# A first expert with 64 slots instead of 128 in a mixture-of-experts stage that streams its weights

## The chip, the cores and the metric

The kernel runs on one core of a Trainium2 chip. The time is device microseconds (us) of that core, the median of several executions of the whole program; less is better. Five engines work side by side: TensorE (PE, with its weight loads as PEld), VectorE (DVE), ScalarE (ACT), GpSimd (POOL) and SyncE (SP), which issues the DMA transfers here.

## The reference

A trunk of two layers over 256 latent tokens and 256 context tokens, model width 1024. The second layer ends with a top-2-of-8 mixture of SwiGLU experts on the 256 latent tokens, and this is the stage of the change:

```python
def _moe(h, router, w1, w3, w2):
    logits = (h @ router).astype(jnp.float32)
    top_v, top_i = lax.top_k(logits, TOP_K)
    weights = jax.nn.softmax(top_v, axis=-1)
    ...
    for e in range(N_EXPERTS):
        out = out + combine[..., e:e + 1] * _swiglu(h, w1[e], w3[e], w2[e])
    return out
```

An expert has three matrices of 1024 x 2816 in fp32, 34.6 MB together; all eight have 277 MB. The arithmetic of the reference on its inputs gives expert 0 54 of the 256 tokens, and the others, from most to least, 115, 83, 79, 58, 50, 46 and 27.

## The kernel before, in words

Only the tokens that chose an expert are computed for it. They are gathered into slots: a token's place in its expert gives a one-hot matrix (`onehot`), and TensorE multiplies the tokens by it (`gather`, tile `pgat`). An expert has either 128 slots ("big") or 64 ("small").

The two kinds are computed in different ways. A **big** expert splits every weight piece of 128x1024 into a high and a low part (`split`: `wh` on ACT, line 154, `wl` on DVE, line 155) and makes three products of 512 columns for each in place of one in full precision (lines 1229 to 1231 up, 1288 to 1290 down). A **small** expert takes the fp32 weights as they were loaded, unsplit, in two halves of 64 slots that lie beside each other in the array (line 1241 up, line 1296 down).

Expert 0 stands at position 0, whatever its count, so that its weights can be loaded before the router is done. The other seven are sorted by their counts (`route_sort`): positions 1 to 3 are big, 4 to 7 small. If more tokens chose an expert than it has slots, `over` is above zero, and a branch at the end computes everything once more for the tokens that were left over. `SEQ` is the order in which the positions are computed.

An expert runs in 11 steps (`NMC`) over its hidden width. A step takes three chunks of weights of 1 MB (tile `mraw`): two for the up product (tile `s`), one for the down product (tile `y`). On PE a step is the up product of this step, then the down product of the step before, then the turn of this step's hidden values (`pht`). The last step of an expert is followed by its combination into the output (`pcmb`), spread over the steps of the next. The gather of the next experts and their weights for the combination (`slots`, tile `ppw`) stand between the steps of a small expert.

The 264 chunks come through one queue on SP in the order of their use, into a ring of 14 buffers (`RINGA` 9, `RINGB` 5): the transfer of a chunk is issued when the buffer of the chunk 14 places ahead has been freed. A small expert frees a chunk when PE has multiplied by it, a big one when it has been split. The first 14 chunks are loaded while the mixer and the router still work. The ids of the experts after position 0 are read from `eid` by SP, ahead of the first chunk of the second expert.

```python
SEQ = (0, 4, 1, 5, 2, 6, 3, 7)
BIG = 4
CAPS = tuple(CAP if p < BIG else HALF for p in range(NE))
```

Of the kernel before, what the change touches and what calls it, by code (L numbers as in the profile page):

```python
# [13 lines left out]
P = 128  # L14
# [3 lines left out]
TC = 256  # L18
# [25 lines left out]

def _moe_order():
    order = []
    for n in range(NMS + 1):
        if n < NMS:
            order += [(n // NMC, n % NMC * 3 + q) for q in range(2)]
        if n:  # L50
            order.append(((n - 1) // NMC, (n - 1) % NMC * 3 + 2))
    return order


MOE_ORDER = _moe_order()


# [74 lines left out]
class Trunk:  # L132
# [808 lines left out]
    def mfetch(self):  # L941
        n = self.mi % len(MOE_ORDER)
        pool = self.mrawa if n % (RINGA + RINGB) < RINGA else self.mrawb
        t = pool.tile([P, MCH], F32, tag="mraw", name="mraw")
        s, j = MOE_ORDER[n]
        if s == 0:
            src = self.wm[j]
        else:
            if s not in self.eids:
                self.eids[s] = self.nc.values_load(  # L950
                    self.eid[0:1, SEQ[s]:SEQ[s] + 1], engines=[mybir.EngineType.SP], min_val=0, max_val=NE - 1,
                    skip_runtime_bounds_check_because="a sum over one row of a permutation of 0 to 7")
            src = self.wm.rearrange("(e j) p m -> e j p m", e=NE)[bass.ds(self.eids[s], 1), j].squeeze(0)
        self.nc.sync.dma_start(t, src)
        self.mi += 1
        self.mq.append(t)
# [55 lines left out]
    def route_end(self):  # L1012
# [49 lines left out]
        for tt, (hi, lo) in enumerate(self.tok):  # L1062
            for hf in range(2):
# [3 lines left out]
                self.order(ins, self.last_oh)  # L1067
        self.gate = self.last_act, ins.name
        return oh
# [62 lines left out]
    def moe(self, X):  # L1132
        tc, nc = self.tc, self.nc
        xe, self.eids = {}, {}
# [4 lines left out]
        def run():  # L1139
            self.experts(X, xe)  # L1140
# [23 lines left out]
    def onehot(self, es, pos=None):  # L1164
        pos = self.poss if pos is None else pos
        oh = []
        for tt in range(2):
            p = self.mp.tile([P, 2, P], F32R, tag="oh", name="oh", bufs=2)
            for q, e in enumerate(es):
                ins = self.nc.vector.tensor_scalar(p[:, q], self.v("iota" if e < BIG else "iota2", 0, P),  # L1170
                                                   pos[:, tt, e:e + 1], None, op0=ALU.is_equal).ins
            oh.append(p.rearrange("p a b -> p (a b)"))
        self.last_oh = ins.name
        for q, e in enumerate(es):
            self.oh[e] = [p[:, q * P:(q + 1) * P].bitcast(F32) for p in oh]
        return oh

    def gather(self, es, xe, oh):
        nc, mp = self.nc, self.mp
        n = P * len(es)  # L1180
        for e in es:
            if e < BIG:
                xe[e] = [(self.mtok if s else mp).tile([P, KD, P], F32R, tag=f"xe{s}", name=f"xe{s}", bufs=XB)
# [3 lines left out]
        for h in range(4):  # L1187
            ks = slice(2 * h, 2 * h + 2)
            for s in range(2):
# [6 lines left out]
                for q, e in enumerate(es):  # L1196
                    if e < BIG:
                        ins = nc.scalar.activation(xe[e][s][:, ks, :], pv[:, q], AF.Copy).ins
                    elif s == 0:
                        nc.scalar.activation(xe[e][:, ks, :], pv[:, q, :, 0:HALF], AF.Copy)  # L1200
                    else:
# [5 lines left out]
    def slots(self, e):  # L1207
# [5 lines left out]
        for tt in range(2):  # L1213
            nc.tensor.matmul(pt[:, TC:TC + NE], p[tt], self.comb[:, tt, :], start=(tt == 0), stop=(tt == 1))
        oht = mp.tile([P, TC], F32R if e < BIG else F32, tag="oht", name="oht", bufs=3)
        nc.vector.tensor_copy(oht, pt[:, 0:TC])
        ws = mp.tile([P, 2], F32, tag="ws", name="ws", bufs=3)
        nc.vector.tensor_copy(ws[:, 0:1], pt[:, TC + e:TC + e + 1])
        return oht, ws[:, 0:1]
# [123 lines left out]

    def experts(self, X, xe):
        pw, py = {}, {}
        self.last_down = None
        steps = [(s, c) for s in range(NE) for c in range(NMC)]
        prev = tail = None
        for n in range(len(steps) + 2):
            if n < len(steps):  # L1350
                s, c = steps[n]
                e = SEQ[s]
                big = e < BIG
                if c == 0:
# [4 lines left out]
                if n == len(steps) - 1:  # L1359
                    self.preload(AF.Sqrt)  # L1360
                if n == 2:
                    pw[e] = self.slots(e)
                at = (c - 4 if s == 0 else c - 1 if not big else -1)
                es = [SEQ[q] for q in (s + 1, s + 2)[:1 if s == 0 else 2] if q < NE]
                if at == 0 and es:
                    oh = self.onehot(es)
                elif at == 2 and es:
                    for _ in self.gather(es, xe, oh):
                        pass
                elif at == 4:  # L1370
                    for q in es:
                        pw[q] = self.slots(q)
                if s == 1 and c == NMC - 1 and self.over is None:
                    self.over = self.nc.values_load(self.cint[0:1, 0:1], min_val=0, max_val=2 * TC)
            else:
                new = None
            if prev:
                pe, pc, ph = prev
                if n == 1:
                    ph = self.turn_big(ph)  # L1380
                big = pe < BIG
# [6 lines left out]
            prev = new if n == 0 else (*new[:2], (self.turn_big if new[0] < BIG else self.turn_small)(new[2])) if new else None  # L1388
        while tail:
# [109 lines left out]
```

## Time and profile before

| | |
|---|---|
| median of 3 runs | 1870.61 us (1870.54 to 1872.69) |
| profiled execution, its own time | 1872.05 us |
| its span, first to last instruction | 1870.3 us |
| mean granted clock of TensorE | 0.991 |
| PE busy | 1831.2 us (98%) |
| DVE busy | 1300.2 us (70%) |
| ACT busy | 889.9 us (48%) |
| chunks of expert weights | 264 of 1024 KB |

The span is what the profiler saw between the first and the last instruction. The share of PE is an average over the whole trunk; the stage of the change is the part from about 1180 us to the end. GB/s in a row is what the core's 16 DMA engines moved together.

### The profile page before, as it was taken

How to read it: one execution, taken by the hardware profiler on the slowest of the kernel's cores; microseconds unless marked ns; L12 is line 12 of the kernel's file. 1: busy time of each engine (PE TensorE's matmuls, PEld its weight loads, DVE VectorE, ACT ScalarE, POOL GpSimd, SP SyncE). 2: the span in 40 equal slices, each digit the busy share in tenths (PEclk: the TensorE clock that was granted, in tenths of full speed). 3: DMA queues.
4: the chain of work that ended last, by engine and by line, in shares of the span. 5: the costliest groups of instructions: out<-in, count | busy, mean ns of one | idle time of the engine just before them, and what ended most of it. 6: DMA issues, size and time to landing. Idle time of an engine off the chain costs nothing.

```text
span 1870.3 us, 26861 instructions
## 1 busy us (share of the span) xinstructions
PE 1831.2 (98%) x10328; PEld 1420.8 (76%) x10328; DVE 1300.2 (70%) x2296; ACT 889.9 (48%) x1259; POOL 0.8 (0%) x6
## 2 busy tenths in 40 slices
PE   7999999999999999999999999999999999999997
PEld 4667777778998888889788998886577668667853
DVE  4899996355679967756999564984298259518932
ACT  3695332253552222235788553773177147416811
POOL 0000000000000000000000000000000000000000
PEclk8999999999999999999999999999999999999999
DMA  8233444231245555421243447789999999999993
GB/s 360 98 142 117 175 180 180 90 135 46 96 161 203 194 183 199 158 90 46 107 153 136 180 181 322 289 339 389 418 420 401 398 419 420 397 407 420 419 397 152
DMA packets 65655, 449.64 MB, mean 240 GB/s; under 512 B 7280, under 2 KB 7408, under 8 KB 23024
## 3 DMA queue, kind: packets, MB, share of 16 engines
q1 hardware_dynamic: 65520, 447.85, 61.1%
q8 instruction: 83, 1.36, 0.3%
q14 instruction: 52, 0.43, 0.1%
HBM read 446.78 MB, written 1.05 MB: 239 GB/s over the span
## 4 chain that ended last, share of the span: by engine, by line
PE 86%; DVE 10%; ACT 2%; DMA 1%; issue 1%; SPq 0%; ACTq 0%; DVEq 0%
PE ps L281 11%; PE ps L283 11%; PE ps L282 11%; PE s L1241 8%; PE s L1231 4%; PE y L1296 4%; PE s L1229 4%; PE s L1230 4%; DVE wl L155 2%; PE y L1290 2%; PE y L1288 2%; PE y L1289 2%; PE ps L780 2%; PE ps L779 2%; PE ps L781 2%; PE pcol L292 1%
## 5 line engine op out<-in xcount | busy, mean ns | idle before, releaser
L154 ACT ACTIVATE wh<-raw 128x1024 fp32r<-128x1024 f32 (+1 forms) x237 | 246.7, 1053 | 453.8 <-PE ps L282 287.1
L155 DVE TENSOR_TENSOR wl<-raw,wh 128x1024 fp32r<-128x1024 f32 (+1 forms) x237 | 286.3, 1215 | 131.5 <-ACT wh L154 129.1
L155 DVE TENSOR_TENSOR wl<-mraw,wh 128x1024 fp32r<-128x1024 f32 x264 | 314.4, 1222 | 29.9 <-ACT wh L154 23.8
L154 ACT ACTIVATE wh<-mraw 128x1024 fp32r<-128x1024 f32 x264 | 272.6, 1057 | 47.2 <-PE s L1230 33.0
L281 PE MATMUL ps<-nh,wh 128*128 128x512 f32 (+1 forms) x736 | 273.3, 371 | 0.7 <-ACT wh L154 0.7
L283 PE MATMUL ps<-nh,wl 128*128 128x512 f32 (+1 forms) x736 | 269.6, 367 | 3.1 <-DVE wl L155 3.1
L282 PE MATMUL ps<-nl,wh 128*128 128x512 f32 (+1 forms) x736 | 269.5, 366 | 0.0
L281 PEld LDWEIGHTS ps<-nh,wh 128*128 128x128 f32 x736 | 139.2, 189 | 30.7 <-issue 2.2
L1241 PE MATMUL s<-mraw,xes 128*64 128x256 f32 x1408 | 162.0, 380 | 0.0
L283 PEld LDWEIGHTS ps<-nh,wl 128*128 128x128 f32 x736 | 139.1, 189 | 27.7 <-DVE wl L155 3.3
L282 PEld LDWEIGHTS ps<-nl,wh 128*128 128x128 f32 x736 | 139.2, 189 | 25.3 <-issue 1.4
L257 ACT ACTIVATE hd<-s 128x256 f32<-128x256 f32 (+1 forms) x88 | 28.8, 328 | 242.5 <-PE s L1241 218.6
L1231 PE MATMUL s<-wl,xe 128*128 128x512 f32 x352 | 139.4, 396 | 4.2 <-DVE wl L155 4.2
L1229 PE MATMUL s<-wh,xe 128*128 128x512 f32 x352 | 142.0, 403 | 0.0
L1230 PE MATMUL s<-wh,xe 128*128 128x512 f32 x352 | 137.8, 392 | 0.0
L1241 PEld LDWEIGHTS s<-mraw,xes 128*64 128x64 f32 x1408 | 98.3, 137 | 44.9 <-issue 0.7
L1250 DVE TENSOR_TENSOR hd<-hd,s 128x256 f32<-128x256 f32 (+1 forms) x88 | 30.9, 351 | 129.9 <-ACT hd L257 129.9
L604 DVE SCALAR_TENSOR_TENSOR cv<-v,vec,cv 128x251 f32<-128x251 f32 (+14 forms) x240 | 102.4, 469 | 0.7
L233 DVE SCALAR_TENSOR_TENSOR junk<-wv,scr 128x512 f32<-128x512 f32 x128 | 84.1, 685 | 0.2
L1231 PEld LDWEIGHTS s<-wl,xe 128*128 128x128 f32 x352 | 66.4, 189 | 23.2 <-DVE wl L155 9.2
L1296 PE MATMUL y<-mraw,hs 128*64 128x512 f32 x352 | 83.4, 595 | 0.4 <-DVE hs L1275 0.4
L1229 PEld LDWEIGHTS s<-wh,xe 128*128 128x128 f32 x352 | 66.6, 189 | 13.0 <-ACT wh L154 0.6
(290 smaller groups left out, 3544.2 us busy)
## 6 DMA issues: line engine op xcount, KB each, us to landing
mraw<-in_wm_dram SPq DMA_DIRECT2D x264, 1024.0 KB, 9.5
raw<-in_wd_dram SPq DMA_DIRECT2D x64, 2048.0 KB, 7.8
wv<-in_wv_dram SPq DMA_DIRECT2D x96, 256.0 KB, 3.6
lw<-in_wd_dram SPq DMA_DIRECT2D x16, 256.0 KB, 2.8
raw<-in_wd_dram SPq DMA_DIRECT2D x2, 1024.0 KB, 14.4
xs<-in_xt_dram SPq DMA_DIRECT2D x1, 1024.0 KB, 4.9
xc<-in_xt_dram SPq DMA_DIRECT2D x1, 1024.0 KB, 7.3
scr<-in_sr_dram SPq DMA_DIRECT2D x4, 256.0 KB, 8.6
```

Of the source, the lines that this page charges most:

```text
L154: return (self.nc.scalar.activation(hi, src, AF.Copy), self.nc.vector.tensor_tensor(lo, src, hi.bitcast(F32), op=ALU.subtract))
L155: self.nc.vector.tensor_tensor(lo, src, hi.bitcast(F32), op=ALU.subtract))
L233: nc.vector.scalar_tensor_tensor(junk, w[h], 1.0, rows[2 * s + h], op0=ALU.mult, op1=ALU.mult, accum_out=acc[:, h, s:s + 1])
L281: self.nc.tensor.matmul(o, wh, ah, start=(k == 0), stop=False)
L282: self.nc.tensor.matmul(o, wh, al, start=False, stop=False)
L283: self.nc.tensor.matmul(o, wl, ah, start=False, stop=(k == KD - 1))
L604: nc.vector.scalar_tensor_tensor(cv[:, a0:a1], v[:, a0 + d:a1 + d], w(t), cv[:, a0:a1], op0=ALU.mult, op1=ALU.add)
L1229: nc.tensor.matmul(p1, xe[0][:, k, :], wh[:, cs], start=(k == 0), stop=False)
L1230: nc.tensor.matmul(p1, xe[1][:, k, :], wh[:, cs], start=False, stop=False)
L1231: nc.tensor.matmul(p1, xe[0][:, k, :], wl[:, cs], start=False, stop=(k == KD - 1))
L1241: nc.tensor.matmul(p1[r, 0:2 * P].rearrange("p (g f) -> p g f", g=2), xe[:, k, :], w[:, :, h * P:(h + 1) * P], start=(k == 0), stop=(k == ...
L1296: ins = self.nc.tensor.matmul(py[0][r, :], hs[:, f * HALF:(f + 1) * HALF], raw[:, f * PIECE + q * 512:f * PIECE + (q + 1) * 512], start=(c ...
```

## The change

Position 0 gets 64 slots: three big positions (1, 2, 3) and five small ones are left. The order becomes small, big, small, big, small, big, small, small. For the overflow there is a second order of nine rounds, `SEQ2`, in which position 0 has two rounds of 128 slots; the branch gathers each expert by itself (`alone`). The order `gate` on the first splits after the gather goes away.

```diff
-SEQ = (0, 4, 1, 5, 2, 6, 3, 7)
-BIG = 4
-CAPS = tuple(CAP if p < BIG else HALF for p in range(NE))
+SEQ = (0, 1, 4, 2, 5, 3, 6, 7)
+BIG = (1, 2, 3)
+CAPS = tuple(CAP if p in BIG else HALF for p in range(NE))
+SEQ2 = (0, NE, 1, 2, 3, 4, 5, 6, 7)
+BIG2 = (0, NE, 1, 2, 3)
...
-        self.gate = self.last_act, ins.name
...
         self.over = None
-        run()
+        run(SEQ)
         with tc.If(self.over > 0):
-            nc.vector.tensor_tensor(self.poss, self.poss,
+            more = self.mp.tile([P, 2, NE + 1], F32, tag="more", name="more")
+            nc.vector.tensor_tensor(more[:, :, 0:NE], self.poss,
                                     self.v("caps", 0, NE).unsqueeze(1).to_broadcast([P, 2, NE]), op=ALU.subtract)
-            for _ in self.gather((0,), xe, self.onehot((0,))):
-                pass
-            run()
+            nc.vector.tensor_scalar(more[:, :, NE], more[:, :, 0], -float(CAP), None, op0=ALU.add)
+            self.poss, self.bigs = more, BIG2
+            run(SEQ2, True)
...
                 at = (c - 4 if s == 0 else c - 1 if not big else -1)
-                es = [SEQ[q] for q in (s + 1, s + 2)[:1 if s == 0 else 2] if q < NE]
+                es = [] if alone else [seq[q] for q in (s + 1, s + 2) if q < NE][:1 if s + 1 < NE and seq[s + 1] not in self.bigs else 2]
```

What this does to the engines' order shows at three places. On PE, right after the first gather, the up product of expert 0 stood as triples of 512 columns; before:

```order
L1193 MATMUL pgat<-oh,tkh 128x128 x4
L1193 MATMUL pgat<-oh,tkl 128x128 x4
L1229 MATMUL s_10534<-wh,xe_10435 128x512
L1230 MATMUL s_10534<-wh,xe_10436 128x512
L1231 MATMUL s_10534<-wl,xe_10435 128x512
L1229 MATMUL s_10534<-wh,xe_10435 128x512
L1230 MATMUL s_10534<-wh,xe_10436 128x512
L1231 MATMUL s_10534<-wl,xe_10435 128x512
```

The same place on PE with the change (its line numbers are 2 higher; `s`, `pht`, `y` and `ppw` as above):

```order
L1195 MATMUL pgat<-oh,tkh 128x128 x4
L1195 MATMUL pgat<-oh,tkl 128x128 x4
L1243 MATMUL s_10532<-mraw,xes 64x256 x16
L1243 MATMUL s_10552<-mraw,xes 64x256 x16
L1271 MATMUL pht<-vec,hd 64x128 x2
L1298 MATMUL y<-mraw,hs 64x512 x4
L1271 MATMUL pht<-vec,hd 64x128 x2
L1243 MATMUL s_10586<-mraw,xes 64x256 x16
L1214 MATMUL ppw<-vec,oh 128x128 x2
```

The products read the loaded chunks (`mraw`) where they read split pieces, and an up product is 16 products of 256 columns for 64 slots where it was 24 of 512 columns.

On DVE after the tokens' low part (`tkl`), the splits of expert 0 (`wl`) stood between the rows of `route_sort`; before:

```order
L1065 TENSOR_TENSOR tkl<-tk,tkh 128x512 x4
L1079 COPY cnt<-ppos 128x8
L155 TENSOR_TENSOR wl<-mraw,wh 128x1024
L1080 TENSOR_TENSOR led<-cnt,vec 128x8
L155 TENSOR_TENSOR wl<-mraw,wh 128x1024
L1084 TENSOR_TENSOR G_10492<-led 128x64
L1085 TENSOR_TENSOR E_10493<-led 128x64
L155 TENSOR_TENSOR wl<-mraw,wh 128x1024
```

The same place on DVE with the change:

```order
L1067 TENSOR_TENSOR tkl<-tk,tkh 128x512 x4
L1080 COPY cnt<-ppos 128x8
L1081 TENSOR_TENSOR led<-cnt,vec 128x8
L1204 TENSOR_TENSOR xes<-xes,pgat 128x128
L1085 TENSOR_TENSOR G_10491<-led 128x64
L1086 TENSOR_TENSOR E_10492<-led 128x64
L1087 TENSOR_TENSOR E_10492<-E_10492,vec 128x64
L1088 TENSOR_TENSOR G_10491<-G_10491,E_10492 128x64
L1204 TENSOR_TENSOR xes<-xes,pgat 128x128
```

The splits are gone from here, and four additions that finish the small expert's gathered tokens (`xes`) have come in.

On PE where the last expert (position 7) begins: before, it followed a big expert, whose last down product and four parts of its combination (`pcmb`, line 1320) stand in its first steps:

```order
L1241 MATMUL s_15631<-mraw,xes 64x256 x16
L1296 MATMUL y<-mraw,hs 64x512 x4
L1320 MATMUL pcmb<-oht,yh 128x256
L1320 MATMUL pcmb<-oht,yl 128x256
L1320 MATMUL pcmb<-oht,yh 128x256
L1320 MATMUL pcmb<-oht,yl 128x256
L1269 MATMUL pht<-vec,hd 64x128 x2
L1241 MATMUL s_15673<-mraw,xes 64x256 x8
```

With the change it follows position 6, a small one, whose combination is one row:

```order
L1243 MATMUL s_15163<-mraw,xes 64x256 x16
L1298 MATMUL y<-mraw,hs 64x512 x4
L1339 MATMUL pcmb<-oht,ys 128x256 x8
L1271 MATMUL pht<-vec,hd 64x128 x2
L1243 MATMUL s_15218<-mraw,xes 64x256 x16
L1298 MATMUL y<-mraw,hs 64x512 x4
L1271 MATMUL pht<-vec,hd 64x128 x2
```

So the last two experts run through one kind of step without a change of kind between them. On SP the order is the same in both: 32 chunks, the read of `eid`, and the rest.

## Rows read from the trace of the kernel before

**Rows 1.** The page: its span, and the chain that ended last by engine.

```profile
span 1870.3 us, 26861 instructions
...
PE 86%; DVE 10%; ACT 2%; DMA 1%; issue 1%; SPq 0%; ACTq 0%; DVEq 0%
```

**Rows 2.** Windows, one an expert: busy us by engine, PEclk, DMA share, GB/s.

```profile
1180.00:1277.00 97.00, 96.89 (x452) 78.83 (x450) 87.80 (x116) 76.33 (x92) 0.00 (x0) 0.99 0.88 335
1277.00:1347.00 70.00, 70.00 (x550) 42.45 (x550) 14.75 (x46) 10.10 (x29) 0.00 (x0) 1.00 1.01 411
1347.00:1444.00 97.00, 95.61 (x430) 75.32 (x428) 85.80 (x94) 70.22 (x85) 0.00 (x0) 1.00 1.01 418
1444.00:1516.00 72.00, 70.61 (x552) 42.22 (x550) 16.41 (x46) 11.66 (x30) 0.00 (x0) 1.00 0.98 396
...
1783.00:1840.00 57.00, 55.63 (x438) 32.41 (x438) 12.73 (x31) 5.96 (x14) 0.00 (x0) 1.00 0.95 386
```

**Rows 3.** Tile mraw: issues (ns min/median/max, first and last start us); issue to landing.

```profile
L954 SPq DMA_DIRECT2D mraw<-in_wm_dram x264: 327/333/642, 1127.1 to 1825.3; - x132
...
DMA to landing us min/median/max: 4.7/9.5/22.8
```

**Rows 4.** Timeline of PE, expert 0 begins: start us, us, instruction.

```profile
1179.52 0.74 PE L1229 MATMUL s<-wh,xe 128*128 128x512 f32 x1
...
1181.76 0.48 PE L1231 MATMUL s<-wl,xe 128*128 128x512 f32 x1
1182.08 0.39 PE L1229 MATMUL s<-wh,xe 128*128 128x512 f32 x1
```

**Rows 5.** Timeline of PE, first up product of positions 4, 5 and 7; in brackets idle before.

```profile
1276.96 3.67 PE L1241 MATMUL s<-mraw,xes 128*64 128x256 f32 x32
...
1444.19 3.67 PE L1241 MATMUL s<-mraw,xes 128*64 128x256 f32 x32
1449.19 0.50 PE L1288 MATMUL y<-wh,hh 128*128 128x512 f32 x1 [1.32 <-ACT wh L154]
...
1782.82 3.67 PE L1241 MATMUL s<-mraw,xes 128*64 128x256 f32 x32
```

**Rows 6.** Timeline of PE, big step: down product begins, two following up products begin.

```profile
1373.76 0.39 PE L1288 MATMUL y<-wh,hh 128*128 128x512 f32 x1
...
1376.63 0.48 PE L1229 MATMUL s<-wh,xe 128*128 128x512 f32 x1
...
1385.06 0.48 PE L1229 MATMUL s<-wh,xe 128*128 128x512 f32 x1
```

**Rows 7.** Timeline of PE, one small step and the next one's start.

```profile
1330.43 3.62 PE L1241 MATMUL s<-mraw,xes 128*64 128x256 f32 x32
1333.88 1.89 PE L1296 MATMUL y<-mraw,hs 128*64 128x512 f32 x8
...
1335.82 3.62 PE L1241 MATMUL s<-mraw,xes 128*64 128x256 f32 x32
```

**Rows 8.** Chain in order of time: start us, us on the chain, work.

```profile
1235.72 3.62 PE pgat L1193 x32
...
1289.12 0.67 PE pcmb L1320 x4
...
1299.81 4.03 PE pgat L1193 x32
...
1366.16 1.92 PE pcmb L1337 x14
```

**Rows 9.** Timeline of PE, slots of two experts, and what follows them.

```profile
1316.34 0.44 PE L1212 MATMUL ppw<-vec,oh 128*128 128x128 f32 x2
...
1317.67 1.94 PE L1296 MATMUL y<-mraw,hs 128*64 128x512 f32 x8
```

**Rows 10.** Timeline of PE, the last down product of the last expert.

```profile
1849.12 1.94 PE L1296 MATMUL y<-mraw,hs 128*64 128x512 f32 x8 [0.39 <-DVE hs L1275]
```

More of the change, by code (lines that the diff above doesn't have):

```diff
@@ L42, with _moe_order @@
 RINGA, RINGB, XB = 9, 5, 1
[L45 to L51, printed above, removed]
+def _moe_order(seq):
+    order, n = [], len(seq) * NMC
+    for m in range(n + 1):
+        if m < n:
+            order += [(seq[m // NMC], m % NMC * 3 + q) for q in range(2)]
+        if m:
+            order.append((seq[(m - 1) // NMC], (m - 1) % NMC * 3 + 2))
     return order
-MOE_ORDER = _moe_order()
+MOE_ORDER = _moe_order(SEQ) + _moe_order(SEQ2)
 def _vec_layout():
@@ L941, in mfetch @@
     def mfetch(self):
-        n = self.mi % len(MOE_ORDER)
+        n = self.mi
         pool = self.mrawa if n % (RINGA + RINGB) < RINGA else self.mrawb
         t = pool.tile([P, MCH], F32, tag="mraw", name="mraw")
-        s, j = MOE_ORDER[n]
-        if s == 0:
+        e, j = MOE_ORDER[n]
+        if e % NE == 0:
             src = self.wm[j]
         else:
-            if s not in self.eids:
-                self.eids[s] = self.nc.values_load(
-                    self.eid[0:1, SEQ[s]:SEQ[s] + 1], engines=[mybir.EngineType.SP], min_val=0, max_val=NE - 1,
+            if e not in self.eids:
+                self.eids[e] = self.nc.values_load(
+                    self.eid[0:1, e:e + 1], engines=[mybir.EngineType.SP], min_val=0, max_val=NE - 1,
                     skip_runtime_bounds_check_because="a sum over one row of a permutation of 0 to 7")
-            src = self.wm.rearrange("(e j) p m -> e j p m", e=NE)[bass.ds(self.eids[s], 1), j].squeeze(0)
+            src = self.wm.rearrange("(e j) p m -> e j p m", e=NE)[bass.ds(self.eids[e], 1), j].squeeze(0)
         self.nc.sync.dma_start(t, src)
@@ L1133, in moe @@
         tc, nc = self.tc, self.nc
-        xe, self.eids = {}, {}
+        xe, self.eids, self.bigs = {}, {}, BIG
         for _ in self.gather((0,), xe, self.route_end()):
@@ L1138, in moe, with run @@
         self.route_weights()
-        def run():
-            self.experts(X, xe)
+        def run(*what):
+            self.experts(X, xe, *what)
             rs = self.rstd_cols(self.colsum(self.square(X, TC, T, "rt"), TC, "rt"), TC)
@@ L1181, in gather @@
         for e in es:
-            if e < BIG:
+            if e in self.bigs:
                 xe[e] = [(self.mtok if s else mp).tile([P, KD, P], F32R, tag=f"xe{s}", name=f"xe{s}", bufs=XB)
@@ L1196, in gather @@
                 for q, e in enumerate(es):
-                    if e < BIG:
+                    if e in self.bigs:
                         ins = nc.scalar.activation(xe[e][s][:, ks, :], pv[:, q], AF.Copy).ins
                     elif s == 0:
-                        nc.scalar.activation(xe[e][:, ks, :], pv[:, q, :, 0:HALF], AF.Copy)
+                        ins = nc.scalar.activation(xe[e][:, ks, :], pv[:, q, :, 0:HALF], AF.Copy).ins
                     else:
@@ L1214, in slots @@
             nc.tensor.matmul(pt[:, TC:TC + NE], p[tt], self.comb[:, tt, :], start=(tt == 0), stop=(tt == 1))
-        oht = mp.tile([P, TC], F32R if e < BIG else F32, tag="oht", name="oht", bufs=3)
+        oht = mp.tile([P, TC], F32R if e in self.bigs else F32, tag="oht", name="oht", bufs=3)
         nc.vector.tensor_copy(oht, pt[:, 0:TC])
         ws = mp.tile([P, 2], F32, tag="ws", name="ws", bufs=3)
-        nc.vector.tensor_copy(ws[:, 0:1], pt[:, TC + e:TC + e + 1])
+        nc.vector.tensor_copy(ws[:, 0:1], pt[:, TC + e % NE:TC + e % NE + 1])
         return oht, ws[:, 0:1]
@@ L1342, in combine_small, with experts @@
         yield
-    def experts(self, X, xe):
+    def experts(self, X, xe, seq, alone=False):
         pw, py = {}, {}
         self.last_down = None
-        steps = [(s, c) for s in range(NE) for c in range(NMC)]
+        steps = [(s, c) for s in range(len(seq)) for c in range(NMC)]
         prev = tail = None
@@ L1351, in experts @@
                 s, c = steps[n]
-                e = SEQ[s]
-                big = e < BIG
+                e = seq[s]
+                big = e in self.bigs
+                if alone and c == 0:
+                    oh = self.onehot((e,))
+                    pw[e] = self.slots(e)
+                    for _ in self.gather((e,), xe, oh):
+                        pass
                 if c == 0:
@@ L1360, in experts @@
                     self.preload(AF.Sqrt)
-                if n == 2:
+                if n == 2 and not alone:
                     pw[e] = self.slots(e)
                 at = (c - 4 if s == 0 else c - 1 if not big else -1)
-                es = [SEQ[q] for q in (s + 1, s + 2)[:1 if s == 0 else 2] if q < NE]
+                es = [] if alone else [seq[q] for q in (s + 1, s + 2) if q < NE][:1 if s + 1 < NE and seq[s + 1] not in self.bigs else 2]
                 if at == 0 and es:
@@ L1369, in experts @@
                         pass
-                elif at == 4:
+                elif at == 4 and es:
                     for q in es:
                         pw[q] = self.slots(q)
-                if s == 1 and c == NMC - 1 and self.over is None:
+                if n == 2 * NMC - 1 and self.over is None:
                     self.over = self.nc.values_load(self.cint[0:1, 0:1], min_val=0, max_val=2 * TC)
@@ L1378, in experts @@
                 pe, pc, ph = prev
+                big = pe in self.bigs
                 if n == 1:
-                    ph = self.turn_big(ph)
-                big = pe < BIG
+                    ph = (self.turn_big if big else self.turn_small)(ph)
                 (self.down_big if big else self.down_small)(py[pe], self.mnext(), ph, pc)
```

4 lines of the change are left out of this document (2 added, 2 removed).

## The prediction

> **What bounds the kernel now.** I read the page first: PE holds 86% of the chain that ended last, DMA 1% [rows 1]. That share covers the whole trunk, so I took the expert stage apart next, with windows cut where one expert ends and the next begins [rows 2]. The reader is to see two things there. PE is busy in every stretch (96.89 of 97 us in expert 0, 70.00 of 70 in position 4). And the DMA engines look just as full (share 0.98 to 1.01 after the first expert), yet move different amounts: 335 GB/s in expert 0, 411 to 418 in the next two, 396 in the fourth. A queue that always had a free buffer to fill would not do that. So PE sets the pace, and the weights are close behind it. A gain on PE counts, until the weights become the later of the two; the sum needs both.
>
> **The first expert, big to small.** Expert 0 runs on PE from 1179.52 [rows 4] to 1276.96 [rows 5], where position 4 begins: 97.4 us. As a small one it would take:
> - 11 steps of 5.39 us (1330.43 to 1335.82), less the last down product and turn, which belong to the next expert's stretch (1333.88 to 1335.82, 1.94 us): 57.4 us [rows 7].
> - One gather for two experts, 4.03 us; before it was for one, 3.62 us [rows 8].
> - Slots: for its own 0.7 and for two 1.3 us (1316.34 to 1317.67 for two [rows 9]).
> - The clock. The granted clock of that stretch is 0.99 [rows 2], and what is missing lies at its start: the first six products take 2.56 us (1179.52 to 1182.08 [rows 4]), where 0.23 us each is usual later (8.43 us a step for 36 of them and a turn, 1376.63 to 1385.06 [rows 6]). That is 1.2 us lost at the lower level, and I leave it the same.
> - The first turn has no other work to hide its copy: 0.4 us, as at the end [rows 10].
>
> Together 65.0 us. The same adding-up for the big expert (11 x 8.43, less 2.87 for the last down product and turn, from 1373.76 to 1376.63 [rows 6], plus 3.62, 1.4 and 1.2) gives 96.1 where the trace has 97.4, so I allow the small one about as much unexplained time and take 66.0: **31.4 us less**.
>
> One rule of the Trainium skill would make this smaller. The rows have 36 products of 512 columns in 8.43 us [rows 6], 0.23 us each. The Trainium skill, "TensorE: Matmul & The Clock Gate" (section "Wait — 56ns, not 53.3ns?"), has products of 512 columns follow each other every 215.7 ns at the full clock; by it a big step would be about 0.55 us shorter, an estimate, and 11 steps would save 6 us less than by the rows. The trace does not agree, and the sum goes by the rows.
>
> The splits of expert 0 leave ACT and DVE (DVE is busy 87.80 of 97 us there, ACT 76.33 [rows 2]). I cost that at nothing, because PE is busy all through that stretch; the cover matters only if PE waits. What comes in on DVE is four additions that complete the gathered tokens, behind some of the sort's small operations. PE needs only the first slice to start, and its first up product takes over 3.45 us [rows 7], so they are hidden. The dropped order on the first splits has nothing left to order.
>
> **The middle.** Before, the stretches between expert 0 and the last were three pairs of small and big, 167.2 us (1276.96 to 1444.19) and twice 169.3 us (1444.19 to 1782.82 [rows 5]). After, they are three pairs of big and small. The later pairs hold a wait of 1.32 us after a big expert (the split of its last down weights is late [rows 5]); the first one does not. With the change every pair has it: 3 x 169.3, less 0.4 because the last of these gathers serves one expert only. That is 507.5 in place of 505.9: **1.6 us more**.
>
> **The last expert.** It takes 66.3 us from its first up product (1782.82 [rows 5]) to its last down product (1849.12 [rows 10]). After a small expert it loses the big combination (4 parts of 0.67 us), the wait of 1.32 us and 0.9 us of the predecessor's down product (2.87 against 1.94), and gains a small combination (14 of its 16 products are 1.92 us, so 2.2 us [rows 8]): **2.7 us less**.
>
> PE alone would then reach its last down product 31.4 - 1.6 + 2.7 = 32.5 us earlier, at 1816.6.
>
> **The weights.** Of 264 chunks the first 14 are there when expert 0 begins. The fifteenth needs a free buffer. A small expert frees one after half an up product, at about 1179.5 + 1.7 + 1.2 = 1182.4, and the soonest landing takes 4.7 us [rows 3]: 1187. The other 249 come at 418 GB/s at best [rows 2], 2.51 us for 1.049 MB: 625 us, so 1812 if the queue never idles. It idles when the ring is full. I count the chunks in hand when each expert begins, 33 being used in each: 14; after expert 0 (58 us of landings, 24 chunks) 5; after position 1 (97 us) 11; after 4 (72 us) 7; after 2, 12; after 5, 8; after 3, 14, which is a full ring; after 6, 9 or less; at the end about 2. So the queue idles only at the end of the second and third big expert. Between none and what a similar stretch shows (396 GB/s for 418 over 72 us, 4 us [rows 2]), I take half of 2 x 4: the last chunk lands at 1816.
>
> That is the same moment as PE's 1816.6. Where two limits meet, small losses of either no longer hide behind the other, and every wait for a chunk in the last two experts costs; I add 2 us and let the last down product begin at 1818.5, which is 30.6 us earlier than now. Behind it the program is unchanged (combination, norm, output).
>
> The sum is made against the span of 1870.3; the profiled execution itself had 1872.05, the median of the runs is 1870.61. I take the difference off the median: **1840.0 us**.
>
> The Trainium skill has a rule that speaks against all this. The rows show 418 GB/s kept up for a whole expert [rows 2]. The Trainium skill, "DMA: Bandwidth & Descriptors" (section "Where 436 GB/s comes from"), says that transfers from HBM are bound by about 358 GB/s a core; by it, as an estimate, 249 chunks would need 729 us and the kernel would become slower by some 66 us. The trace does not bear this out.
>
> **The rivals.**
> 1. The weights are the bound and eat part of the gain: the queue keeps 411 GB/s (its rate in position 4, at share 1.01 [rows 2]; 2.55 us a chunk, 635 us) and idles the full 8 us. The last chunk lands at 1830, the change is 18 us, the time 1852. For it: two small experts in a row at the end use 66 chunks in about 130 us, where 52 can land. Against it: 14 buffers stand in front of them.
> 2. The weights eat the gain whole and more. The last down product stays at 1849.1 if the chunks come every 2.66 us, 394 GB/s; below that the kernel is slower than before. At the 386 GB/s of the last stretch [rows 2] it would be 2.72 us a chunk, 677 us, and the last down product would stand at 1864 and the time at 1885. Against it: that stretch includes the end of the transfers, and the lower rates stand where the ring had been full. This decides only if the queue is slow with free buffers, and no row shows that.
> 3. The branch runs. Expert 0 has 54 tokens by the reference's arithmetic; from 65 on the nine rounds of the branch follow, five big (97 us) and four small (72 us), some 775 us: about 2615 us. Ten tokens lie between, and the other small positions (58 at most) are as they were.
> 4. More gain than I take: the small first expert takes 65.0, the queue never idles, no losses where the limits meet. The last down product begins at 1815.6, the time is 1837; with no idle copy or clock loss either, 1835.
>
> **How the numbers follow.** The forecast (1835 to 1847) gets 0.72, rival 1 (1847 to 1860) 0.16, rival 2 0.04, rival 3 0.02, rival 4 below 1835 0.06. The range takes in the forecast, rival 4's bound and rival 1's centre: 1833 to 1853, which leaves out 0.06 for rivals 2 and 3 and about a tenth for the tails. A run of this kernel can tell 0.2%, 3.7 us, from no change. Faster: 0.95; within 0.2%: 0.01 (rival 2 near 394 GB/s); slower: 0.04.
>
> **What would show it.** In the profile after, position 1's first up product (512 columns, with split weights) begins at about 1246 instead of 1277; the windows of that first small expert show 400 GB/s or more where 335 stood; each of the three big-small pairs lasts about 169 us; in the last two experts PE has short waits for chunks, together under 6 us, and the last down product begins between 1815 and 1822. It would be wrong in the sum of PE if the first small stretch takes over 70 us with PE busy, for instance with the lower clock lasting; wrong in the weights if PE waits over 10 us for chunks in the last experts; wrong altogether if `mraw` has more than 264 issues.

## The result, and the profile after

The changed kernel takes 1849.83 us (median of 4 runs, 1846.87 to 1851.57), the kernel before in the same measurement 1870.88: ratio 0.9883, 95% interval 0.9871 to 0.9895. It is faster by 21 us where 30.6 were forecast. The time lies inside the range, 9.8 us above the number. The profiled execution took 1851.57 us.

The page of the changed kernel, its span, PE's busy time, and the chain that ended last [rows 1 for before]:

```profile
span 1849.5 us, 26754 instructions
...
PE 1805.6 (98%) x10394; PEld 1380.3 (75%) x10394; DVE 1220.4 (66%) x2232; ACT 815.0 (44%) x1177; POOL 0.8 (0%) x6
...
PE 80%; DVE 11%; DMA 5%; ACT 2%; issue 1%; SPq 0%; ACTq 0%; DVEq 0%
```

PE lost 25.6 us of work (1831.2 before), the span 20.8. What is missing shows in the chain, where DMA rose from 1% to 5%: at some place the end now hangs on a chunk. Windows with one expert each [rows 2] (first, second and third expert, last one):

```profile
1180.00:1247.00 67.00, 66.60 (x527) 39.83 (x523) 11.46 (x46) 9.96 (x28) 0.00 (x0) 0.96 0.95 382
1247.00:1345.00 98.00, 96.61 (x428) 75.11 (x427) 86.04 (x94) 70.46 (x85) 0.00 (x0) 1.00 1.01 419
1345.00:1417.00 72.00, 70.62 (x549) 42.44 (x550) 16.43 (x46) 11.00 (x30) 0.00 (x0) 1.00 1.00 400
...
1758.00:1828.00 70.00, 64.03 (x504) 35.86 (x500) 9.52 (x30) 5.23 (x14) 0.00 (x0) 1.00 0.98 405
```

PE is busy through every expert but the last, where 6 of 70 us are idle. The first small expert moves 382 GB/s where 335 stood, yet the small one behind a big one only 400, at a DMA share of 1.00. The timeline of PE where these experts begin, and at the last down product [rows 4, 5, 10]:

```profile
1179.55 9.70 PE L1243 MATMUL s<-mraw,xes 128*64 128x256 f32 x64
...
1246.96 0.50 PE L1231 MATMUL s<-wh,xe 128*128 128x512 f32 x1
...
1345.85 3.67 PE L1243 MATMUL s<-mraw,xes 128*64 128x256 f32 x32
...
1757.98 3.62 PE L1243 MATMUL s<-mraw,xes 128*64 128x256 f32 x32
...
1828.50 1.94 PE L1298 MATMUL y<-mraw,hs 128*64 128x512 f32 x8 [0.38 <-DVE hs L1277]
```

The terms of the forecast against these rows, in us:

| | forecast | after |
|---|---|---|
| first expert | 66.0 | 67.4 |
| the six between | 507.5 | 511.0 |
| last expert | 63.6 | 70.5 |
| where the limits meet | 2.0 | in the rows above |
| first expert begins to last down product | 639.0 | 649.0 |

Before, that last distance was 669.6 (1179.52 to 1849.12 [rows 4, 10]). The ten us too much have three places; the largest is the last expert. What PE waited for from position 7's first product on (waits: place, releaser, us in total, times, longest):

```profile
PE s L1243 <- DMA mraw<-in_wm_dram: 3.5, 7, 1.2
PE y L1298 <- DMA mraw<-in_wm_dram: 1.7, 3, 0.6
PE pcmb L1339 <- ACT ys L1331: 0.8, 1, 0.8
PE y L1298 <- DVE hd L1252: 0.6, 1, 0.6
```

With the wait for `hd`, which follows on a late up product, chunks cost 5.8 us. The chain in order of time says the same from the other side: two chunks of 20 us each follow each other to the last step.

```profile
1785.57 19.76 DMA mraw<-in_wm_dram
...
1805.45 20.38 DMA mraw<-in_wm_dram
...
1825.96 1.94 PE y L1298 x8
```

Why the queue is late shows in windows of 15 us around the ends of big experts (1345.85, 1516.53 and 1687.21); columns here are us, PEclk, DMA share, GB/s:

```profile
1320.00:1335.00 15.00, 1.00 1.01 420
...
1350.00:1365.00 15.00, 1.00 1.00 374
...
1505.00:1520.00 15.00, 1.00 0.93 359
1520.00:1535.00 15.00, 1.00 0.97 355
...
1690.00:1705.00 15.00, 1.00 0.94 342
```

Away from these joints the queue keeps 420 GB/s, a chunk every 2.49 us. At each of the three joints it falls to between 342 and 374. From the first chunk that needed a freed buffer (landed at 1188.1) to the last (1828.3) there are 249 intervals; 249 x 2.49 is 620, so 20 us were lost where the forecast had 4 (15 by the forecast's own 2.51 us a chunk).

The loss comes before all 14 chunks are in. For each landing I counted how many issued transfers were still under way: after the landings that left only one or two (50 of 249), the next came 0.29 us later than 2.49 on average, 14.6 us together; with four or more it came within 0.05 us of 2.49 on average. The view of the tile `mraw` has the reason [rows 3]:

```profile
L956 SPq DMA_DIRECT2D mraw<-in_wm_dram x264: 327/333/671, 1126.8 to 1807.9; - x132
...
DMA to landing us min/median/max: 4.8/11.6/22.7
```

A chunk lands 4.8 us after its issue at the soonest, so one alone under way cannot give one each 2.49 us, and two only just can. This reading fits the counts; no run set the number of transfers under way by itself. The Trainium skill, "DMA: Bandwidth & Descriptors" (section "Anatomy of one DMA — SWDGE (gpsimd) path"), splits a transfer into about 2.0 us that are fixed and the bytes at 436 GB/s; by it, as an estimate, 1 MB takes 4.4 us. It speaks of another path than SP's queue, and the 4.8 us here are near it.

### The profile page after: what moved, and what is told of

The parts are those of the page before. It is cut to its first block, busy times and chain, and to the rows that moved or that the text cites. A ratio compares the mean times of both kernels' runs of the same rounds, so it can differ in the third digit from the quotient of the medians.

```text
span 1849.5 us, 26754 instructions
## 1 busy us (share of the span) xinstructions
PE 1805.6 (98%) x10394; PEld 1380.3 (75%) x10394; DVE 1220.4 (66%) x2232; ACT 815.0 (44%) x1177; POOL 0.8 (0%) x6
## 4 chain that ended last, share of the span: by engine, by line
PE 80%; DVE 11%; DMA 5%; ACT 2%; issue 1%; SPq 0%; ACTq 0%; DVEq 0%
PE ps L283 11%; PE ps L285 11%; PE ps L284 11%; PE s L1243 8%; DMA mraw<-in_wm_dram 4%; PE y L1298 4%; PE s L1233 3%; PE s L1232 3%; PE s L1231 3%; DVE wl L157 2%; PE y L1292 2%; PE y L1291 2%; PE y L1290 2%; PE ps L782 2%; PE ps L781 2%; PE ps L783 2%
## 5 line engine op out<-in xcount | busy, mean ns | idle before, releaser
L157 DVE TENSOR_TENSOR wl<-mraw,wh 128x1024 fp32r<-128x1024 f32 x198 | 234.0, 1222 | 24.9 <-ACT wh L156 23.8
L156 ACT ACTIVATE wh<-mraw 128x1024 fp32r<-128x1024 f32 x198 | 202.8, 1055 | 30.1 <-PE s L1232 23.6
L1243 PE MATMUL s<-mraw,xes 128*64 128x256 f32 x1760 | 205.3, 384 | 3.6 <-DMA mraw<-in_wm_dram 3.5
L1243 PEld LDWEIGHTS s<-mraw,xes 128*64 128x64 f32 x1760 | 124.6, 138 | 62.4 <-DMA mraw<-in_wm_dram 4.3
L259 ACT ACTIVATE hd<-s 128x128 f32<-128x128 f32 (+1 forms) x88 | 27.9, 317 | 304.4 <-PE s L1243 279.8
L1252 DVE TENSOR_TENSOR hd<-hd,s 128x128 f32<-128x128 f32 (+1 forms) x88 | 29.6, 336 | 174.1 <-ACT hd L259 174.1
L1233 PE MATMUL s<-wl,xe 128*128 128x512 f32 x264 | 104.9, 397 | 4.2 <-DVE wl L157 4.2
L1298 PE MATMUL y<-mraw,hs 128*64 128x512 f32 x440 | 104.5, 595 | 3.2 <-DMA mraw<-in_wm_dram 1.7
L1231 PE MATMUL s<-wh,xe 128*128 128x512 f32 x264 | 106.6, 404 | 0.0
L1232 PE MATMUL s<-wh,xe 128*128 128x512 f32 x264 | 103.7, 393 | 0.0
L283 PE MATMUL pglu<-nh,wh 128*128 128x256 f32 (+1 forms) x192 | 64.6, 337 | 1.0 <-ACT wh L156 1.0
```

Source lines behind the costliest of these rows:

```text
L156: return (self.nc.scalar.activation(hi, src, AF.Copy), self.nc.vector.tensor_tensor(lo, src, hi.bitcast(F32), op=ALU.subtract))
L157: self.nc.vector.tensor_tensor(lo, src, hi.bitcast(F32), op=ALU.subtract))
L283: self.nc.tensor.matmul(o, wh, ah, start=(k == 0), stop=False)
L1231: nc.tensor.matmul(p1, xe[0][:, k, :], wh[:, cs], start=(k == 0), stop=False)
L1232: nc.tensor.matmul(p1, xe[1][:, k, :], wh[:, cs], start=False, stop=False)
L1233: nc.tensor.matmul(p1, xe[0][:, k, :], wl[:, cs], start=False, stop=(k == KD - 1))
```

## The experiments

Theory W: two small experts in a row use 66 chunks faster than they come, and the idle queue at the joints had emptied the ring before them. Rival Q: the queue is too slow for the whole stage. Theory S: the big steps' extra time comes from where the tiles lie in memory. Rival X: it is an accident of the execution. The stage is the time from the first expert's first product to the last down product; waits are those for chunks, with `hd` behind them; spacing is the mean time between starts of 512-column products in a row, up and down. All but the time and the ratio are of the profiled execution. Each ratio is against the kernel before as timed beside that run, with medians of 1870.88 to 1872.23. Stages differ by up to 1.1 us for the length of the first expert alone, which follows its clock (see the section on the prediction).

| run | time, us | ratio, 95% interval | stage, us | waits, us | spacing, ns |
|---|---|---|---|---|---|
| before | 1870.88 | | 669.6 | 0 | 229 / 227 |
| changed | 1849.83 | 0.9883 [0.9871, 0.9895] | 649.0 | 5.8 | 231 / 234 |
| e1_order | 1844.82 | 0.9856 [0.9840, 0.9873] | 643.1 | 1.4 | 231 / 234 |
| e2_ring13 | 1852.07 | 0.9900 [0.9884, 0.9917] | 650.9 | 7.1 | 231 / 234 |
| e3_ring15 | 1846.65 | 0.9872 [0.9855, 0.9888] | 644.6 | 3.4 | 231 / 234 |
| e6_layout | 1845.86 | 0.9863 [0.9847, 0.9880] | 643.8 | 5.7 | 229 / 227 |
| e7_ws4 | 1849.44 | 0.9874 [0.9858, 0.9889] | 649.7 | 5.6 | 233 / 232 |
| e10_ws8 | 1845.45 | 0.9858 [0.9842, 0.9874] | 643.6 | 6.1 | 229 / 227 |
| e11_ws11 | 1850.00 | 0.9877 [0.9861, 0.9893] | 648.8 | 5.6 | 231 / 234 |
| e8_best | 1843.42 | 0.9849 [0.9829, 0.9869] | 640.8 | 0 | 233 / 232 |
| e12_order_ws8 | 1841.63 | 0.9833 [0.9819, 0.9846] | 639.6 | 2.2 | 229 / 227 |
| e4_four_big | 1878.77 | 1.0040 [1.0026, 1.0054] | 676.8 | 0 | 231 / 234 |

### Order and ring: e1_order, e2_ring13, e3_ring15

```diff
-SEQ = (0, 1, 4, 2, 5, 3, 6, 7)
+SEQ = (0, 1, 4, 2, 5, 6, 3, 7)
```

```diff
-RINGA, RINGB, XB = 9, 5, 1
+RINGA, RINGB, XB = 9, 4, 1
```

The first diff is e1_order, the second e2_ring13. e3_ring15 has 9, 6, 1 there; it also lets the sort's tiles `G2` and `E2` share the memory of `G` and `E`, to make room.

> Only the order changes: position 6 before position 3, so that the two small experts in a row stand in the middle and a big one lies between them and the last. Theory W (the 7 us by which the last expert is slower than its products come from chunks that are not there yet, because the queue stood idle at a full ring behind the big experts, and two small experts in a row use more than arrives): the ring still has chunks left at the small pair, the big expert behind it fills it again, PE waits for chunks under 1.5 us in all, and the time falls by 4 to 7 us, to 1843 to 1846. Rival Q (the queue is simply too slow for what small experts ask, wherever they stand): the same 6 us of waits move to the pair in the middle, and the time stays within 2 us of 1850. Both expect the big steps at 8.55 us as in the changed kernel.

> The ring has 13 buffers in place of 14, nothing else. W: one chunk less in hand where the small experts begin, and the queue idle earlier behind each big expert; waits for chunks in the last two experts grow from 6 to 8 to 13 us, the time rises by 2 to 7 us, to 1852 to 1857. Q: the rate of the queue sets the end, a buffer more or less changes only one chunk's head start, 2.5 us at most, and the last chunk lands no later than 1831. A third reading, that PE sets the end and the waits are covered: within 1 us of 1850.

> The ring has 15 buffers (the sort's small tiles share buffers with the router's to make room), nothing else. W: the waits in the last two experts shrink from 6 to 1 to 4 us and the queue is idle less; the time falls by 2 to 5 us, to 1845 to 1848. Q: at most one chunk's head start, 2.5 us. The tiles move by 8192 bytes together: if the big steps stay at 8.55 us, such a shift does not matter to them; a step of 8.43 us would say that it does.

The waits of the three, whole stage (e1_order, then e2_ring13, then e3_ring15, whose lines are one higher):

```profile
PE s L1231 <- ACT wh L156: 1.3, 1, 1.3
...
PE s L1243 <- DMA mraw<-in_wm_dram: 0.8, 2, 0.5
...
PE y L1298 <- DMA mraw<-in_wm_dram: 0.6, 1, 0.6
```

```profile
PE s L1243 <- DMA mraw<-in_wm_dram: 4.0, 10, 0.5
PE y L1298 <- DMA mraw<-in_wm_dram: 2.5, 4, 0.6
```

```profile
PE s L1244 <- DMA mraw<-in_wm_dram: 1.6, 4, 0.5
PE y L1299 <- DMA mraw<-in_wm_dram: 1.2, 2, 0.6
```

Q falls: the 6 us of waits do not move to the pair in the middle, the time falls by 5.0 us, and the last expert, now behind a big one, waits for no chunk. The stage is 5.9 us shorter; 3.9 of them are idle time of PE, 0.8 the first expert's clock, and the rest is not assigned. W holds in part. The pair in the middle still runs out of chunks at its end: besides the 1.4 us PE waits 1.3 us for the first split of the big expert behind it, whose chunk was late (first line; ACT waits for `mraw` there), so 2.7 us in all. The pair also gets its chunks no faster: from its start there are 12 in hand and 54 landings in 140 us, in both kernels. What spares it most of the waits is probably work on PE that W does not name. Its second expert gathers for the two experts behind it (4.1 us) and makes their slots (1.3 us), which the last expert of the changed kernel has no cause to do; the first row of each in e1_order:

```profile
1606.12 0.74 PE L1195 MATMUL pgat<-oh,tkh 128*128 128x256 f32 x4
...
1621.41 0.44 PE L1214 MATMUL ppw<-vec,oh 128*128 128x128 f32 x2
```

No run moved this work without the order, so its share stays open. One buffer fewer or more moves the waits by +1.3 and -2.4 us and the time by +2.2 and -3.2, in W's direction. For fewer the effect is smaller than W's 8 to 13 us of waits, and it does not tell W from Q: the last chunk landed at 1828.9, as Q allowed. The added waits are all in the last expert.

### The places of the tiles: e6_layout, e7_ws4, e10_ws8, e11_ws11

The granted clock is 1.00 in the big experts before and after, yet a big step takes 8.55 to 8.58 us instead of 8.43 [rows 6 for before], and a big expert 98.9 instead of 97.5. Two following up products of the changed kernel:

```profile
1277.17 0.48 PE L1231 MATMUL s<-wh,xe 128*128 128x512 f32 x1
...
1285.74 0.48 PE L1231 MATMUL s<-wh,xe 128*128 128x512 f32 x1
```

The first expert's kind changes the order in which tiles are first asked for, and with it where the tiles lie that PE holds still in a big expert: `xe0` from 120416 to 132032, `hh` from 127840 to 136128, `hlo` from 129888 to 138176 (bytes in a partition; the split weights stay at 84320 and up). e6_layout asks for them in the old order:

```diff
+        if not self.eids and not xe:
+            for tag, w, bufs in (("xe0", KD * P, XB), ("pad", 320, 1), ("hd", 256, 2), ("hh", 256, 2), ("hlo", 256, 2),
...
+                    nc.gpsimd.memset(mp.tile([P, w], F32, tag=tag, name="lay", bufs=bufs)[:, 0:2], 0.0)
```

The other three only shift them, by the number of buffers of a small tile:

```diff
-        ws = mp.tile([P, 2], F32, tag="ws", name="ws", bufs=3)
+        ws = mp.tile([P, 2], F32, tag="ws", name="ws", bufs=8)
```

That is e10_ws8; e7_ws4 has 4 there, e11_ws11 11.

> The tiles of the expert stage are claimed in the order of the kernel before, so that the big experts' gathered tokens, hidden values and one-hot matrices lie at the addresses that they had there; the program is otherwise the changed one. Theory S (the big steps take 8.55 us in the changed kernel and 8.43 us before because their stationary tiles lie elsewhere): the step is back at 8.43 us, 1.3 us less an expert and 4 us less on PE; since the last chunks set the end, most of that turns into longer waits for chunks, and the time falls by 0 to 3 us. Rival X (a difference from one execution to the next, or from the queue's traffic beside it): the step stays at 8.55 us here, and varies among the kernels that have the changed kernel's addresses.

> The changed kernel with one more buffer for the small tile ws (three to four, 8 bytes a buffer, 32 bytes as they are laid out); the work, the order and the ring are unchanged. It shifts the tiles that PE holds still in a big expert by 32 bytes: xe0 from 132032 to 132064, hh from 136128 to 136160, hlo from 138176 to 138208, so that each stands 32 bytes past a multiple of 64 again, as before the change, but some 10 KB from where it stood then. Theory S64 (what makes the big steps slower is where in 64 bytes these tiles begin): a big step takes 8.43 us again, up products start 227 to 229 ns apart and down products 227 ns, and the time is as with the old places, 1844 to 1848. Rival P (it is the neighbourhood in memory, such as which tiles share a stretch with xe and hh): 231 and 234 ns as in the changed kernel, big steps of 8.55 us, 1848 to 1852.

> The changed kernel with eight buffers for ws in place of three: 160 bytes more ahead of xe0, hh and hlo, which begin at 132192, 136288 and 138336. That is 96 bytes past a multiple of 256 for each, as it was before the change (120416, 127840, 129888) and as it is for the split weights that PE reads beside them (84320, 92512, 96608, ...); in the changed kernel it was 192, with one more buffer of ws 224. Theory S256 (what counts is where the tiles stand in 256 bytes): products start 227 to 229 ns apart, a big step takes 8.43 us, a big expert 97.5, the time as with the old places, 1844 to 1848. Rival P2 (the region of memory counts, not the place in 256 bytes, since these tiles stay some 12 KB from where they were): 231 to 235 ns, 1848 to 1852.

> The control: eleven buffers for ws, 256 bytes more than in the changed kernel, so xe0, hh and hlo begin at 132288, 136384 and 138432, again 192 past a multiple of 256. Theory S256: 231 ns between up products and 234 between down products, as in the changed kernel, and 1848 to 1852. Rival P2, or any effect that is only one of distance: something else than these two numbers, and if distance from the old place alone slowed it, no less than they.

The timeline of PE, eleven down products in a row of the changed kernel, of e10_ws8, of e11_ws11 and of e7_ws4; the last row holds two, and the tenth step ends at its start:

```profile
1299.92 0.40 PE L1290 MATMUL y<-wh,hh 128*128 128x512 f32 x1
...
1302.27 0.63 PE L1292 MATMUL y<-wl,hh 128*128 128x512 f32 x2
```

```profile
1296.00 0.39 PE L1290 MATMUL y<-wh,hh 128*128 128x512 f32 x1
...
1298.27 0.62 PE L1292 MATMUL y<-wl,hh 128*128 128x512 f32 x2
```

```profile
1299.79 0.40 PE L1290 MATMUL y<-wh,hh 128*128 128x512 f32 x1
...
1302.14 0.63 PE L1292 MATMUL y<-wl,hh 128*128 128x512 f32 x2
```

```profile
1299.89 0.39 PE L1290 MATMUL y<-wh,hh 128*128 128x512 f32 x1
...
1302.21 0.63 PE L1292 MATMUL y<-wl,hh 128*128 128x512 f32 x2
```

Ten spacings are 2.35, 2.27, 2.35 and 2.32 us. S holds, and X falls: the old places give the old spacing and 4.0 us less time. That is more than the 0 to 3 us that e6_layout was expected to give: the waits stayed at 5.7 us and did not grow, and its last chunk landed at 1823.4, 4.9 us sooner than in the changed kernel. The queue moved with PE, so it did not set the end by itself. My first reading of S, that the place within 64 bytes counts, fell with e7_ws4: 32 bytes restored that, and products came every 233 and 232 ns, a third pattern with the longest big steps of all (8.60 us). With 160 bytes (place 96 in 256, as before the change) the old spacing came back, far from the old places; with 256 bytes more than in the changed kernel the changed kernel's own spacing did, to the nanosecond. In e3_ring15, where by its expectation all these tiles lie 8192 bytes further on, a multiple of 256, the spacing stayed as well. So the place within 256 bytes tells the spacing in every case that was tried (96, 192 and 224). Whatever is laid out behind `ws` moves with the three tiles; that it is these three is likely, because PE reads them in these products, but not shown apart. That the split weights also stand at 96 suggests that the two together count; no run moved the weights by themselves, so this stays open.

### What the gain is: e4_four_big

```diff
-SEQ = (0, 1, 4, 2, 5, 3, 6, 7)
-BIG = (1, 2, 3)
+SEQ = (0, 1, 5, 2, 6, 3, 7, 4)
+BIG = (1, 2, 3, 4)
```

> The changed kernel with position 4 big as well, and so four big experts as before the change, but the first one small: small, big, small, big, small, big, small, big. Theory (the gain is that of one big expert fewer on PE, whichever it is): nearly all of it goes. Before had 1871; big steps slowed by the places of their tiles add 44 x 0.12 = 5 us, the end behind a big expert adds its combination and about 3 us of last down products: 1873 to 1880. Rival (the gain comes from a small expert being first: it needs no split, lets go of its chunks sooner and starts the queue earlier): with as much of it as 10 us, below 1862. PE waits for no chunk by the first, since four big experts leave the queue time.

The timeline of PE, first part of its last down product:

```profile
1854.64 0.73 PE L1290 MATMUL y<-wh,hh 128*128 128x512 f32 x2 [0.47 <-ACT hh L156]
```

The first expert is small, no chunk is waited for, and the kernel is slower than before. Four big experts, each 1.4 us longer than before, make 5.5 of the 7.2 us that its stage is longer. So the gain is that of one big expert fewer; that the first one is small, and needs no split, gives nothing that is seen.

### The third rival's price: e9_overflow

```diff
-    put("caps", np.tile(np.array(CAPS, f32), (P, 1)))
+    put("caps", np.tile(np.array((48,) + CAPS[1:], f32), (P, 1)))
```

> The changed kernel with the limit of position 0 in the overflow's test set from 64 to 48 slots, so that its 54 tokens are over the limit and the branch runs; tokens 49 to 54 of expert 0 are then counted twice in the output. It measures the third rival's price, put at 775 us. Nine rounds, five big (97 to 99 us) and four small (70 to 72) are 765 to 783; each gathers by itself between two experts (4 us in the open, five of which were hidden or shared before, some 15 us), and the first chunks of the branch come only after its test: 5 to 25 us. Sum 785 to 825, so 2635 to 2675. If the nine rounds are bound by the weights instead (297 chunks at 2.5 us are 743), no more than this either. Should PE wait for chunks between rounds, since small and big gathers in the open let the queue go on, it would show as more than 10 us of waits for mraw.

It took 2674.68 us, one run. The timeline of PE, the last down product ahead of the branch, its first work, and the last down product in it:

```profile
1824.72 1.94 PE L1298 MATMUL y<-mraw,hs 128*64 128x512 f32 x8 [0.38 <-DVE hs L1277]
...
1840.12 0.66 PE L1214 MATMUL ppw<-vec,oh 128*128 128x128 f32 x2 [3.15 <-DVE oh L1172]
...
2653.98 1.94 PE L1298 MATMUL y<-mraw,hs 128*64 128x512 f32 x8 [0.38 <-DVE hs L1277]
```

The branch costs 829 us, where the rival had 775. Counted from one round's `ppw` to the next one's, the five big rounds take 100 to 103 us and the first three small ones 69, 74 and 84; the fourth takes 83 to its last down product. The last two are 33 chunks of 2.49 us (82) and little more: with four small rounds in a row the weights set the pace. The waits from the branch's start:

```profile
PE s L1243 <- DMA mraw<-in_wm_dram: 16.5, 38, 1.4
PE y L1298 <- DMA mraw<-in_wm_dram: 8.7, 14, 0.6
```

That is 25 us of waits, more than the 10 that the expectation took as its limit. None comes before 2450: they stand in the second to fourth small round, and not at the gathers between big rounds.

### Both causes taken away: e8_best, e12_order_ws8

e8_best is e1_order's order, e3_ring15's ring and e7_ws4's 32 bytes; e12_order_ws8 is e1_order's order and e10_ws8's 160 bytes, with the ring of 14.

> The changed kernel with three edits together: position 6 computed ahead of position 3 (small, big, small, big, small, small, big, small), a ring of 15 buffers, and the 32 bytes of ws. If the theories W (two small experts in a row at the end meet an emptied ring) and S64 (places of the tiles) are both right, their gains nearly add: with the order alone 1844.8, of which 1.8 us were waits for chunks that the 15th buffer removes, and 33 big steps of 0.12 us less give 4: about 1839, 1837 to 1842, with waits for chunks under 1 us. If S64 is wrong it stays at 1843 (1841 to 1845). If the weights rather than PE set the end (rival Q), the last chunk does not land earlier than with the order alone, at 1822, and the time stays above 1843.

> Position 6 ahead of position 3 and the eight buffers of ws together, with the ring of 14. If S256 holds, the order's 1844.8 less 33 big steps of 0.12 us: about 1841, 1839 to 1843, with a little more waiting for chunks at the two small experts in the middle, since big experts that are shorter leave the queue less time (2 to 4 us). If S256 is wrong, 1843 to 1846.

e8_best has no wait of PE for a chunk, only 0.4 us for a split behind a late one, but the slow spacing; its runs spread over 10 us (1837.69 to 1847.3), and its median is that of "S64 is wrong". e12_order_ws8 has the lowest median; its interval overlaps with e8_best's. Its windows around the fourth to sixth experts, and its last down product:

```profile
1416.00:1514.00 98.00, 96.64 (x440) 76.21 (x442) 85.76 (x94) 70.17 (x85) 0.00 (x0) 1.00 1.01 417
1514.00:1586.00 72.00, 70.63 (x558) 42.20 (x556) 15.62 (x44) 7.32 (x19) 0.00 (x0) 1.00 1.00 405
1586.00:1655.00 69.00, 66.19 (x526) 38.81 (x522) 12.80 (x40) 9.27 (x26) 0.00 (x0) 1.00 1.01 420
```

```profile
1818.79 1.94 PE L1298 MATMUL y<-mraw,hs 128*64 128x512 f32 x8 [0.38 <-DVE hs L1277]
```

The two small experts in a row now stand between big ones; the second of them lets the queue run at 420 GB/s, and PE waits 2.2 us for chunks in all, and 1.3 us for the split of a late one. The two gains nearly add: 5.0 us from the order, 4.4 from the bytes, 8.2 together.

## Why the prediction was right, and where it was off

- **The sign and the mechanism** were right: one big expert fewer, of which PE saves a big part, and weights that come close behind. e4_four_big shows that it is this and nothing about being first.
- **The first expert** was forecast at 66.0 and took 67.4. The term that was small is the clock: 1.2 us were allowed for, but in this execution the granted clock stayed at its lower level (0.50, which is 1.2 GHz) until about 1185, with PE busy throughout, as the windows show; the fourth row is the kernel before, where it was at 1.00 from 1182 on:

```profile
1179.00:1182.00 3.00, 3.00 (x15) 1.91 (x17) 1.61 (x8) 2.86 (x4) 0.00 (x0) 0.50 0.00 0
1182.00:1185.00 3.00, 3.00 (x18) 1.62 (x16) 0.07 (x1) 0.00 (x0) 0.00 (x0) 0.53 0.39 55
1185.00:1188.00 3.00, 3.00 (x30) 1.95 (x28) 0.29 (x1) 0.28 (x1) 0.00 (x0) 1.00 0.91 369
...
1182.00:1185.00 3.00, 3.00 (x14) 2.46 (x14) 2.26 (x7) 2.27 (x3) 0.00 (x0) 1.00 0.00 0
```

  That is 5.4 us at the lower level, about half of it lost, an estimate. In eight of the other kernels the clock rose sooner after the expert's start and the same expert took 66.2 to 66.7; in e2_ring13, e7_ws4 and e11_ws11 it rose as late and the expert took 67.3 to 67.4. The 66.0 lie just below all of them.
- **The middle** was forecast at 507.5 and took 511.0. The step that failed is "3 x 169.3", which takes the big step over from before at 8.43 us: three big experts of 98.9 us instead of 97.5 are 4.1 us more. Nothing in the diff names it; the order of first requests moved tiles to another place in 256 bytes. With the old place the big expert takes 97.5 us again (e10_ws8: 1243.62 to 1341.16).
- **The last expert** was forecast at 63.6 plus the 2.0 where the limits meet, and took 70.5. The wait for chunks was 5.8 us, just inside "together under 6 us". The term behind it, the queue's idle time, was mis-sized: 4 us forecast, 20 measured. The count of chunks in hand was close at first (12 when position 4 begins, 11 forecast), but not at the end: 12 when position 6 begins, where 14 were forecast, and 5 when position 7 begins, where the forecast had "9 or less". The step that failed is "it idles when the ring is full", and only behind the second and third big expert: the queue was slower already when only one or two transfers were under way, which happened around the end of all three. So the last chunk landed at 1828.3 instead of 1816; some 5 of these 12 us go back to the slower big steps, since it landed at 1823.4 in e6_layout.
- **The range and the signs.** The time lies in the band of rival 1 (1847 to 1860), which had 0.16, and not in the forecast's own (1835 to 1847), which had 0.72; the range holds it because it reaches to rival 1's centre. All three misses go the same way, and the one of the middle was no term of the sum. Of the signs, position 1's start (1246.96), the pairs (169.6 to 170.7 us) and the waits came as said; the first small expert moved 382 GB/s and not 400, and the last down product began at 1828.50 and not between 1815 and 1822.
- **The rivals.** The first, weights that eat part of the gain (1852, last chunk at 1830), came close in time and in its last chunk, but by another way: the pace stayed at 2.49 us a chunk where it had 2.55, and the idle time was 20 us where it had 8. The second did not occur: 420 GB/s was kept where several transfers were under way, and the loss of some 66 us that the prediction weighed did not come. The third did not occur, and costs 54 us more than it said. The fourth's 1837 is no run's median; but with the two causes gone (e12_order_ws8) the stage takes 639.6 us, where the forecast had 639.0, and the time is 1841.63 for 1840.0.

## What to carry to other kernels

Where two limits lie within 1% of each other, count a ring not as full or empty but by the transfers under way: with a soonest landing of 4.8 us and a pace of 2.49, landings with fewer than three under way already came late here, and where the fast users of the ring stand, and what other work stands among them, was worth more here (5.0 us) than one more buffer (3.2 us). When a change alters which tiles are asked for first, compare the spacing of products that the change doesn't touch, before looking for the loss in what it does touch: a few bytes of padding may give it back.

## What was not expected of the hardware

The spacing of 512-column products goes with where the held operand begins in memory: 227 ns for down products with it 96 bytes past a multiple of 256, 234 ns at 192, 232 ns at 224, at the same granted clock of 1.00. At 192 it is 3% of a down product's spacing and 1.4% of a big expert (98.9 us for 97.5). The Trainium skill, "SBUF — State Buffer" (section "Operand start alignment"), asks only that an operand start at a multiple of its element's size, and says that it speaks of what is allowed and not of speed; nothing here contradicts that, and the three spacings are what the place costs in speed.
